# The first two gate/up blocks of a two-layer decoder as plain products in two token halves, and another order of the seven products of the 2x2 form

## The chip, the cores and the metric

The kernel runs on one core of one Trainium2 chip. The metric is the device time of one execution in microseconds (us), the median of three runs. The engines are named as the profile names them: PE does matmuls (PEld loads their weights), DVE, ACT and POOL do elementwise work, SP issues the DMAs from HBM. Matmuls write into PSUM banks; everything else lives in SBUF.

## The reference

Two layers over 512 tokens of width 1024. A layer is a token mixer, a LayerNorm over the residual sum, a SwiGLU feed-forward, a second LayerNorm, and a gated input embedding. All of it is fp32. The change touches the seam between the mixer's LayerNorm and the feed-forward's first product:

```python
x = layer_norm(DEEPNORM_ALPHA * x + h, ln_mix_g[i], ln_mix_b[i])          # h: the mixer's output, o @ w_o
x = layer_norm(DEEPNORM_ALPHA * x + swiglu_ffn(x, ffn_w_in[i], ffn_w_down[i]), ln_ffn_g[i], ln_ffn_b[i])
...
def swiglu_ffn(x, w_in, w_down):
    h = x @ w_in                       # (512 x 1024) @ (1024 x 5632)
    g, u = h[..., :D_FF], h[..., D_FF:]    # D_FF = 2816
    return (jax.nn.silu(g) * u) @ w_down
```

Layer 0 mixes by latent attention, layer 1 by a gated linear recurrence (HGRN2); both end with a product `o @ w_o` of 1024 x 1024.

## The kernel before, in words

**Precision.** Every fp32 operand is split into a high and a low part (`split`, lines 177 to 179: the high part by ACT, the low part by a subtraction on DVE, or on POOL where the caller says so), and a product is three matmuls (`mm3`, lines 190 to 195: high by high, high by low, low by high). So there are no single matmuls in what follows, only threes.

**The mixer's last product** (`out_proj`) runs over the four 128-token tiles t = 0 to 3, with tokens on the partitions. After the second 512 columns of a tile comes its LayerNorm: the sums (L318), mean (L324, L325), squared deviations on ACT (L326), the reciprocal root on POOL (`rstd`, L203: the power -0.5 of a 128x1 tile), and two passes over the tile in two halves each (L331, L335). Each half is then put on a list. `flush` takes the list: four PE transposes into one bank (L297), and the `sink` of `Winograd` makes the operands of the next product from that bank. `rows` calls `flush` after the matmuls of the next token tile, so tile t's transposes stand on PE behind tile t+1's matmuls. What is left on the list after the last tile (tile 2's and tile 3's halves) is flushed inside `gate_up`.

**gate/up** computes 22 blocks j of 128 gate and 128 up columns each, transposed (the 128 columns on the partitions, the 512 tokens along the row). Gate and up together, and the two token halves, make a 2x2 product of 2x2 quarters over the 1024 inner columns, and it is done with seven quarter products where eight would be plain. With A11, A12 (inner halves of tokens 0 to 255) and A21, A22 (of tokens 256 to 511), the sink makes S1 = A21 + A22, S2 = S1 - A11, S3 = A11 - A21 and S4 = A12 - S2; `prep(j)` (L380 to L401) loads the block's two 128x1024 weight units ra and rb and makes T1 (L389), half of T3 (L390), T2 (L391) and T4 (L392), each with its split. `product` is 12 matmuls of 128x256. A block is thus 84 matmuls.

The functions are recorded instruction by instruction; `prep(j)` is called ahead of block j, and a scheduler places the recorded work on the engines by its dependencies and by the tile pools. A tile of a pool must be free before its next owner may be written: raw weights have 3 buffers, whi and wlo 5 each, the middle-sized tiles `ma` and `mb` 5 each, PSUM has 3 banks `ps`, 2 `sc`, 2 `tp`, 1 `wg`. On an engine, instructions run in the order that the program gives.

**The seam.** Blocks 0 and 1 are written as generators that take turns: A11 and A12 of block 0, then `flush` (tile 2), the same of block 1 with `flush` (tile 3), A22 of both, and then the rest of both. A11 and A12 need tokens 0 to 255 alone, so they may run before tiles 2 and 3 are through their LayerNorm. From block 2 on the order is A11, S1, A12, S2, A22, S4, S3. Products into one bank accumulate: A11 with S2 and S3 into A; S1 with S4 into C. A copy of the bank (L416, ACT) is taken between them, and the sums with the copies (L424, L451, L454, L455 on DVE), the two silus on ACT (L425, L456) and the two products on POOL (L452, L457) make the block's 128 rows of h.

## Time and profile before

| what | us |
|---|---|
| median of three runs | 1347.09 |
| lowest and highest | 1346.31, 1347.42 |
| the profiled execution's own time | 1346.94 |
| its span, from the first to the last instruction | 1345.2 |
| PE busy in the span | 1286.0 (96%) |
| DVE, ACT, POOL busy | 905.9, 615.2, 328.3 |

The mean granted TensorE clock is 0.984 of full speed. Over the whole span PE is the engine that is nearly always busy, but an average hides stages; what the change touches are two short stretches, one per layer, where the mixer ends and gate/up begins: about 177 to 263 us and, 724.7 us later, 902 to 988 us. "Idle before" a row is the time for which its engine waited ahead of that instruction, and the arrow names what released it. Rows with a line of `mm3` (L193 to L195) say which product they belong to by the operand and the bank.

### The profile page before, as it was taken

To read this page: it belongs to the slowest core of one execution; us is meant where nothing else is said; L and a number is where in the kernel's file an instruction comes from. 1 tells how busy PE (TensorE), PEld (TensorE's weight loads), DVE (VectorE), ACT (ScalarE), POOL (GpSimd) and SP (SyncE) were. 2 spreads that over 40 slices of the span, in tenths; PEclk is the share of its full clock that TensorE was granted. 3 is DMA by queue.
4 is the path that set the end of the run, shared out by engine and by line. 5 is a ranking of instruction groups with operands and counts; after the bars stand their busy time and mean duration, and the time that the engine had idled before them with its cause. 6 is when DMAs were issued, how large, how long until landed. Compare 5 with 4: busy or idle time off the path is not lost.

```text
span 1345.2 us, 20010 instructions
## 1 busy us (share of the span) xinstructions
PE 1286.0 (96%) x7852; PEld 1144.8 (85%) x7852; DVE 905.9 (67%) x1396; ACT 615.2 (46%) x1080; POOL 328.3 (24%) x259
## 2 busy tenths in 40 slices
PE   8999978899999999999999999996899999999998
PEld 8787867899999888888888887886899999888887
DVE  7988398889884433753377776369789895633473
ACT  6666255555654333533334434235455554422352
POOL 0200034566552000100002220023566663100000
PEclk9999998999999999999999999997999999999999
DMA  6213102333332432331422220321333332433321
GB/s 220 79 48 126 47 32 95 110 111 95 110 110 71 142 101 95 97 119 64 126 62 64 63 63 29 129 72 39 126 95 98 122 96 64 157 96 105 97 91 51
DMA packets 36095, 125.00 MB, mean 93 GB/s; under 512 B 4384, under 2 KB 4640, under 8 KB 35744
## 3 DMA queue, kind: packets, MB, share of 16 engines
q1 hardware_dynamic: 36000, 123.71, 28.4%
q8 instruction: 62, 1.02, 0.3%
q14 instruction: 33, 0.27, 0.1%
HBM read 121.60 MB, written 2.10 MB: 92 GB/s over the span
## 4 chain that ended last, share of the span: by engine, by line
PE 82%; DVE 9%; issue 3%; POOL 3%; ACT 2%; DMA 1%; SPq 0%; DVEq 0%; POOLq 0%; ACTq 0%
PE ps L194 18%; PE ps L193 18%; PE ps L195 18%; PE sc L193 3%; PE sc L194 3%; PE sc L195 3%; PE wg L194 3%; PE wg L195 3%; PE wg L193 3%; PE tp L297 2%; DVE wlo L179 2%; PE sc L803 2%; PE tp L195 1%; PE tp L193 1%; PE tp L194 1%
## 5 line engine op out<-in xcount | busy, mean ns | idle before, releaser
L179 DVE TENSOR_TENSOR wlo<-raw,whi 128x1024 fp32r<-128x1024 f32 (+1 forms) x167 | 204.7, 1228 | 83.2 <-ACT whi L178 81.2
L193 PE MATMUL ps<-big,whi 128*128 128x256 f32 (+1 forms) x688 | 217.7, 316 | 20.8 <-ACT big L178 6.0
L178 ACT ACTIVATE whi<-raw 128x1024 fp32r<-128x1024 f32 (+1 forms) x171 | 177.1, 1038 | 111.2 <-PE ps L194 52.2
L195 PE MATMUL ps<-big,wlo 128*128 128x256 f32 (+1 forms) x688 | 216.5, 315 | 1.2 <-DVE wlo L179 1.2
L194 PE MATMUL ps<-big,whi 128*128 128x256 f32 (+1 forms) x688 | 215.1, 313 | 2.5 <-DVE big L179 2.5
L193 PE MATMUL ps<-whi,big 128*128 128x512 f32 (+2 forms) x440 | 171.0, 389 | 0.0
L195 PE MATMUL ps<-whi,big 128*128 128x512 f32 (+2 forms) x440 | 168.7, 383 | 0.0
L194 PE MATMUL ps<-wlo,big 128*128 128x512 f32 (+2 forms) x440 | 168.4, 383 | 0.0
L193 PEld LDWEIGHTS ps<-big,whi 128*128 128x128 f32 x688 | 133.8, 194 | 28.1 <-ACT big L178 6.6
L194 PEld LDWEIGHTS ps<-big,whi 128*128 128x128 f32 x688 | 133.7, 194 | 8.5 <-DVE big L179 3.1
L195 PEld LDWEIGHTS ps<-big,wlo 128*128 128x128 f32 x688 | 133.7, 194 | 6.8 <-DVE wlo L179 1.6
L203 POOL TENSOR_TENSOR rr<-rv,mhalf 128x1 f32<-128x1 f32 (+2 forms) x28 | 26.8, 958 | 424.7 <-DVE rv L201 424.7
L195 PEld LDWEIGHTS ps<-whi,big 128*128 128x128 f32 x440 | 83.1, 189 | 15.5
L179 DVE TENSOR_TENSOR ma<-big,ma 128x512 fp32r<-128x512 f32 x40 | 28.5, 717 | 100.4 <-ACT ma L178 100.4
L194 PEld LDWEIGHTS ps<-wlo,big 128*128 128x128 f32 x440 | 83.3, 189 | 14.4
L193 PEld LDWEIGHTS ps<-whi,big 128*128 128x128 f32 x440 | 83.2, 189 | 14.3
L390 POOL TENSOR_TENSOR ma<-raw,raw 128x512 f32<-128x512 f32 x44 | 87.8, 1994 | 0.0
L179 DVE TENSOR_TENSOR mb<-ma,mb 128x1024 fp32r<-128x1024 f32 x44 | 76.8, 1744 | 15.0 <-PE wg L194 15.0
L178 ACT ACTIVATE ma<-big 128x512 fp32r<-128x512 f32 x40 | 25.2, 630 | 122.6 <-PE wg L195 120.4
L389 POOL TENSOR_TENSOR ma<-raw 128x512 f32<-128x512 f32 x44 | 60.9, 1383 | 79.3 <-DVE wlo L179 63.4
L391 DVE TENSOR_TENSOR ma<-ma,raw 128x512 f32<-128x512 f32 x44 | 65.6, 1490 | 19.1 <-POOL ma L389 16.6
L457 POOL TENSOR_TENSOR big<-part,part 128x256 f32<-128x256 f32 x40 | 59.7, 1493 | 54.8 <-ACT part L456 54.8
(299 smaller groups left out, 3273.3 us busy)
## 6 DMA issues: line engine op xcount, KB each, us to landing
raw<-ffn_w_in SPq DMA_DIRECT2D x88, 512.0 KB, 3.6
raw<-ffn_w_down SPq DMA_DIRECT2D x44, 512.0 KB, 3.5
raw<-ple_w_gate SPq DMA_DIRECT2D x16, 512.0 KB, 3.5
raw<-hgrn_w_fq SPq DMA_DIRECT2D x16, 512.0 KB, 3.5
raw<-mla_w_o SPq DMA_DIRECT2D x8, 512.0 KB, 3.5
big<-ln SPq DMA_DIRECT2D x8, 512.0 KB, 4.8
raw<-hgrn_w_v SPq DMA_DIRECT2D x8, 512.0 KB, 4.7
raw<-hgrn_w_g SPq DMA_DIRECT2D x8, 512.0 KB, 3.5
```

What stands on the lines that cost most here:

```text
L178: self.nc.scalar.activation(hi, src, AF.Copy)
L179: (eng or self.nc.vector).tensor_tensor(out=lo, in0=src, in1=hi.bitcast(F32), op=ALU.subtract)
L193: mm(ps, a[0], b[0], start=start, stop=False, skip_group_check=more)
L194: mm(ps, a[0], b[1], start=False, stop=False, skip_group_check=more)
L195: mm(ps, a[1], b[0], start=False, stop=stop, skip_group_check=more)
L203: nc.gpsimd.tensor_tensor(out=r, in0=v, in1=self.mhalf[:, :n], op=ALU.pow)
L297: self.nc.tensor.transpose(out=ps[:, c * P:(c + 1) * P], in_=src[:, c * P:(c + 1) * P], identity=self.ident)
L389: nc.gpsimd.tensor_tensor(out=ta[:, up], in0=rb[:, up], in1=rb[:, lo], op=ALU.subtract)
L390: nc.gpsimd.tensor_tensor(out=ta[:, lo], in0=rb[:, lo], in1=ra[:, lo], op=ALU.subtract)
L391: v.tensor_tensor(out=tb[:, lo], in0=ta[:, up], in1=ra[:, lo], op=ALU.add)
L457: nc.gpsimd.tensor_tensor(out=h[:, N:], in0=u1, in1=g1, op=ALU.mult)
L803: nc.tensor.matmul(ps[:, c * P:(c + 1) * P], X[:, c * P:(c + 1) * P], pair_view(cs[0][:, :, 1, :], cs[1][:, :, 0, :]), start=True, stop=True)
```

## The change

`plain(h, w, half)` computes one token half of one block without the 2x2 form: gate and up, eight 128-wide inner pieces each, three matmuls of 128x256 for a piece, so 48 matmuls for a half and 96 for a block, where the 2x2 form has 84. Blocks 0 and 1 are computed so: tokens 0 to 255 of block 0, `flush`, the same of block 1, `flush`, then tokens 256 to 511 of both. Their weights come as four `unit`s whose low parts are made on POOL; `prep` is called for blocks 2 to 21 only. Since plain products of tokens 256 to 511 need A21, which the 2x2 form doesn't, the sink also splits A21 (one more ACT and one more DVE instruction of 128x512 for tiles 2 and 3 each). The sink's last subtraction, S4, goes from POOL to DVE. The LayerNorm parameters of the mixer stand in two `ma` tiles in place of a 14-slot pool's slot; the freed slot holds the A21 split. From block 2 on the order of products is A11, A12, S1, S2, A22, S4, S3.

Lines of the kernel after are 1 to 18 higher than before: L193 to L195 become L194 to L196, L203 becomes L204, L179 becomes L180, L331 and L335 become L334 and L338, L389 to L392 become L392 to L395, L451 becomes L453.

```diff
--- before.py
+++ after.py
@@ -106,14 +106,15 @@
         self.b = b
         two = lambda: [b.slot([P, 2, 4, 256], F32R) for _ in range(2)]
         self.a1, self.s13, self.s24 = two(), two(), two()
-        self.a22 = b.slot([P, 2, 4, 256], F32R)
+        self.a2 = [b.slot([P, 2, 4, 256], F32R) for _ in range(2)]
         self.raw = [b.mid([P, 4, 256]) for _ in range(2)]
         self.at = {}
 
     def __call__(self, name):
 
-        if name == "A22":
-            return self.a22[:, 0], self.a22[:, 1]
+        if name in ("A21", "A22"):
+            z = self.a2[name == "A22"]
+            return z[:, 0], z[:, 1]
         z, n = {"A11": (self.a1, 0), "A12": (self.a1, 1), "S1": (self.s13, 0), "S3": (self.s13, 1),
                 "S2": (self.s24, 0), "S4": (self.s24, 1)}[name]
         return z[0][:, n], z[1][:, n]
@@ -125,6 +126,7 @@
             b.split(self.a1[0][:, n, :, cs], self.a1[1][:, n, :, cs], ps)
             nc.scalar.activation(self.raw[n][:, :, cs], ps, AF.Copy)
             return
+        b.split(self.a2[n][:, 0, :, cs], self.a2[n][:, 1, :, cs], ps)
         if n == 0:
             a21 = b.small([P, 4, P], tag="t2", bufs=T2)
             nc.scalar.activation(a21, ps, AF.Copy)
@@ -136,8 +138,7 @@
         sy = b.mid([P, 2, 4, P], tag="mb")
         nc.vector.tensor_tensor(out=sx[:, 0], in0=ps, in1=a21, op=ALU.add)
         nc.vector.tensor_tensor(out=sy[:, 0], in0=ps, in1=sx[:, 1], op=ALU.subtract)
-        b.split(self.a22[:, 0, :, cs], self.a22[:, 1, :, cs], ps)
-        nc.gpsimd.tensor_tensor(out=sy[:, 1], in0=self.raw[1][:, :, cs], in1=sy[:, 0], op=ALU.subtract)
+        nc.vector.tensor_tensor(out=sy[:, 1], in0=self.raw[1][:, :, cs], in1=sy[:, 0], op=ALU.subtract)
         b.split(self.s13[0][:, :, :, cs], self.s13[1][:, :, :, cs], sx)
         b.split(self.s24[0][:, :, :, cs], self.s24[1][:, :, :, cs], sy)
 
@@ -306,11 +307,13 @@
         self.pend = []
 
 
-    def ln_params(self, idx):
-        gb = self.slot([P, 2, D])
+    def ln_params(self, idx, slot=False):
+        if slot:
+            z = self.slot([P, 2, D])
+        gb = (z[:, 0], z[:, 1]) if slot else (self.mid([P, D]), self.mid([P, D]))
         for n in range(2):
-            self.nc.sync.dma_start(gb[:, n], self.i["ln"][2 * idx + n])
-        return gb[:, 0], gb[:, 1]
+            self.nc.sync.dma_start(gb[n], self.i["ln"][2 * idx + n])
+        return gb
 
     def ln_half(self, x, t, n, ps, st):
 
@@ -405,13 +408,27 @@
                 self.mm3(ps[:, :N], [z[:, kc * P:(kc + 1) * P] for z in t], [z[:, kc] for z in s],
                          kc == 0 and not more, kc == 3, more)
 
-        def block(j):
-            w = prep(j)
+        def out(j):
             if j < 20 and j % 4 == 0:
                 hT.append(self.slot([P, 4, S]))
             elif j == 20:
                 hT.append(self.mid([P, 2, S]))
-            h = hT[j // 4][:, j % 4]
+            return hT[j // 4][:, j % 4]
+
+        def plain(h, w, half):
+
+            ps = [self.bank(), self.bank()]
+            for q in range(2):
+                for kc in range(KC):
+                    self.mm3(ps[q][:, :N], [z[:, kc * P:(kc + 1) * P] for z in w[q]],
+                             [z[:, kc % 4] for z in xT(f"A{half + 1}{kc // 4 + 1}")], kc == 0, kc == KC - 1)
+            g = self.small([P, N], tag="part", bufs=7)
+            nc.scalar.activation(g, ps[0][:, :N], AF.Silu)
+            v.tensor_tensor(out=h[:, half * N:(half + 1) * N], in0=ps[1][:, :N], in1=g, op=ALU.mult)
+
+        def block(j):
+            w = prep(j)
+            h = out(j)
             part = lambda: self.small([P, N], tag="part", bufs=7)
             copy = lambda dst, src: nc.scalar.activation(dst, src[:, :N], AF.Copy)
             A, B = self.bank(), self.bank("sc")
@@ -419,34 +436,19 @@
             product(A, xT("A11"), w["B11"])
             copy(g0, A)
 
-            def p2():
-                product(B, xT("A12"), w["B21"])
-                v.tensor_tensor(out=g0, in0=B[:, :N], in1=g0, op=ALU.add)
-                nc.scalar.activation(g0, g0, AF.Silu)
-
-            def p4():
-                d = self.bank("wg")
-                product(d, xT("A22"), w["T4"])
-                g1 = part()
-                copy(g1, d)
-                return g1
-
-            if j < 2:
-                p2()
-                self.flush()
-                yield
-                g1 = p4()
-                yield
+            product(B, xT("A12"), w["B21"])
+            v.tensor_tensor(out=g0, in0=B[:, :N], in1=g0, op=ALU.add)
+            nc.scalar.activation(g0, g0, AF.Silu)
             C = self.bank()
             u0, u1 = part(), part()
             product(C, xT("S1"), w["T1"])
             copy(u1, C)
-            if j >= 2:
-                p2()
             product(A, xT("S2"), w["T2"], True)
             copy(u0, A)
-            if j >= 2:
-                g1 = p4()
+            d = self.bank("wg")
+            product(d, xT("A22"), w["T4"])
+            g1 = part()
+            copy(g1, d)
             product(C, xT("S4"), w["B22"], True)
             v.tensor_tensor(out=u0, in0=C[:, :N], in1=u0, op=ALU.add)
             nc.gpsimd.tensor_tensor(out=h[:, :N], in0=u0, in1=g0, op=ALU.mult)
@@ -455,20 +457,21 @@
             v.tensor_tensor(out=u1, in0=A[:, :N], in1=u1, op=ALU.add)
             nc.scalar.activation(g1, g1, AF.Silu)
             nc.gpsimd.tensor_tensor(out=h[:, N:], in0=u1, in1=g1, op=ALU.mult)
-            yield
-
-        first = [block(0), block(1)]
-        for _ in range(3):
-            for b in first:
-                next(b)
+
+
+        hs = [out(j) for j in range(2)]
+        ws = [[self.unit(win[j, q], True) for q in range(2)] for j in range(2)]
+        for half in range(2):
+            for j in range(2):
+                plain(hs[j], ws[j], half)
+                self.flush()
         for j in range(2, NF):
-            for _ in block(j):
-                pass
+            block(j)
         return hT
 
     def ffn(self, l, x, xT, ln):
         hT = self.gate_up(l, xT)
-        gb = self.ln_params(ln)
+        gb = self.ln_params(ln, True)
         yT = Pair(self)
         acc = [(self.bank(f), self.bank(g)) for f, g in (("tp", "tp"), ("sc", "sc"), ("ps", "ps"), ("ps", "wg"))]
         NL = 3
```

Two places show how the instructions stand. The first is POOL at the seam of layer 0. rr is the reciprocal root of a LayerNorm (in these rows the four tiles of the mixer's, in order), wlo a weight unit's low part, ma<-raw the two subtractions of `prep`, mb<-ma the sink's S4. Before:

```order
L203 TENSOR_TENSOR rr_1944<-rv_1942,mhalf 128x1
L203 TENSOR_TENSOR rr_1998<-rv_1996,mhalf 128x1
L389 TENSOR_TENSOR ma_2128<-raw_2121 128x512
L390 TENSOR_TENSOR ma_2128<-raw_2121,raw_2120 128x512
L389 TENSOR_TENSOR ma_2208<-raw_2201 128x512
L390 TENSOR_TENSOR ma_2208<-raw_2201,raw_2200 128x512
L203 TENSOR_TENSOR rr_2052<-rv_2050,mhalf 128x1
L140 TENSOR_TENSOR mb_2097<-ma_1752,mb_2097 128x512
L203 TENSOR_TENSOR rr_2114<-rv_2112,mhalf 128x1
L140 TENSOR_TENSOR mb_2190<-ma_1752,mb_2190 128x512
```

and now:

```order
L180 TENSOR_TENSOR wlo_2128<-raw_2125,whi_2127 128x1024
L204 TENSOR_TENSOR rr_1946<-rv_1944,mhalf 128x1
L204 TENSOR_TENSOR rr_2000<-rv_1998,mhalf 128x1
L204 TENSOR_TENSOR rr_2054<-rv_2052,mhalf 128x1
L180 TENSOR_TENSOR wlo_2134<-raw_2131,whi_2133 128x1024
L180 TENSOR_TENSOR wlo_2140<-raw_2137,whi_2139 128x1024
L180 TENSOR_TENSOR wlo_2146<-raw_2143,whi_2145 128x1024
L392 TENSOR_TENSOR ma_2395<-raw_2388 128x512
L393 TENSOR_TENSOR ma_2395<-raw_2388,raw_2387 128x512
L204 TENSOR_TENSOR rr_2118<-rv_2116,mhalf 128x1
```

The first row's low part is plain block 0's. Three more of them now stand behind tile 2's reciprocal root (rr_2054); then come block 2's two subtractions (L392, L393), and tile 3's reciprocal root (rr_2118) stands behind these. Before, tile 3's (rr_2114) had only S4 of tile 2 ahead of it. raw_2388 is the second weight unit of block 2; its buffer is the one that plain block 1's first unit (raw_2137, read by wlo_2140) leaves.

The second place is DVE in the same stretch, from tile 2's LayerNorm to tile 3's. big_1741 holds tiles 2 and 3 of the residual, tp are transposed tiles, ps_2004 and now ps_2006 tile 2's last product, ps_2060 tile 3's. Before:

```order
L391 TENSOR_TENSOR ma_2129<-ma_2128,raw_2120 128x512
L179 TENSOR_TENSOR ma_2134<-raw_2121,ma_2134 128x512
L318 SCALAR_TENSOR_TENSOR big_1741,lnst_1758<-big_1741,ps_2004 128x512
L392 TENSOR_TENSOR ma_2129<-ma_2129,raw_2120 128x512
L179 TENSOR_TENSOR big_1745<-tp_2029,big_1744 128x4x128
L179 TENSOR_TENSOR big_1745<-tp_2037,big_1744 128x4x128
L324 TENSOR_TENSOR lnst_1758<-lnst_1758 128x1
L325 TENSOR_SCALAR lnst_1758<-lnst_1758 128x1
L179 TENSOR_TENSOR wlo_2138<-ma_2128,whi_2137 128x1024
L201 TENSOR_SCALAR rv_2050<-lnst_1758 128x1
L331 SCALAR_TENSOR_TENSOR big_1741<-big_1741,lnst_1758,big_1753 128x512 x2
L335 SCALAR_TENSOR_TENSOR big_1741<-big_1741,rr_2052,big_1753 128x512 x2
```

and now:

```order
L321 SCALAR_TENSOR_TENSOR big_1741,lnst_1760<-big_1741,ps_2006 128x512
L327 TENSOR_TENSOR lnst_1760<-lnst_1760 128x1
L328 TENSOR_SCALAR lnst_1760<-lnst_1760 128x1
L180 TENSOR_TENSOR big_1745<-tp_2031,big_1744 128x4x128
L180 TENSOR_TENSOR big_1745<-tp_2039,big_1744 128x4x128
L202 TENSOR_SCALAR rv_2052<-lnst_1760 128x1
L334 SCALAR_TENSOR_TENSOR big_1741<-big_1741,lnst_1760,ma_1754 128x512 x2
L338 SCALAR_TENSOR_TENSOR big_1741<-big_1741,rr_2054,ma_1755 128x512 x2
L321 SCALAR_TENSOR_TENSOR big_1741,lnst_1761<-big_1741,ps_2060 128x512
L327 TENSOR_TENSOR lnst_1761<-lnst_1761 128x1
L328 TENSOR_SCALAR lnst_1761<-lnst_1761 128x1
L180 TENSOR_TENSOR big_1750<-tp_2085,big_1750 128x4x128
```

Before, block 0's weight work (L391, ma_2134, L392, wlo_2138) stood among tile 2's steps; now its sums, mean and passes follow each other with only tile 1's two splits between them, and its own splits (tp_2085) come after tile 3's mean. Further on the same engine, the second half of tile 3's second pass and block 2's preparation now stand thus:

```order
L338 SCALAR_TENSOR_TENSOR big_1741<-big_1741,rr_2118,ma_1755 128x512
L427 TENSOR_TENSOR big_2124<-ps_2150,part_2199 128x256
L180 TENSOR_TENSOR big_1750<-tp_2202,big_1750 128x4x128
L180 TENSOR_TENSOR wlo_2392<-raw_2387,whi_2391 128x1024
L134 TENSOR_TENSOR mb_2211<-ma_1752,tp_2202 128x512
L180 TENSOR_TENSOR big_1751<-tp_2213,big_1751 128x4x128
L139 TENSOR_TENSOR mb_2211<-tp_2213,t_420_2209 128x512
L140 TENSOR_TENSOR mb_2220<-tp_2213,mb_2211 128x512
L427 TENSOR_TENSOR big_2124<-ps_2229,part_2278 128x256
L141 TENSOR_TENSOR mb_2220<-ma_1753,mb_2220 128x512
L180 TENSOR_TENSOR big_1747<-mb_2211,big_1746 128x8x128
L394 TENSOR_TENSOR ma_2396<-ma_2395,raw_2387 128x512
```

The row that waits for tile 3's reciprocal root (rr_2118) has plain block 0's product with silu (L427), block 2's first low part (wlo_2392) and the whole sink of tile 3 (tp_2202, tp_2213) behind it, and only then comes block 2's T2 (L394).

On PE, tile 2's transposes now stand directly behind tile 3's 24 matmuls; then come plain block 0's 48 matmuls, 14 of plain block 1's in layer 0 (24 in layer 1), tile 3's first four transposes, the rest of that half with the other four among it, and the 96 matmuls of the second halves. Before, 11 matmuls of block 0 stood ahead of tile 2's transposes, and tile 3's stood behind A11 and A12 of blocks 0 and 1.

## The prediction

> **What bounds the kernel now.** I read the page's shares first: PE is busy for 96% of the span, so only what shortens PE's work or its waits can help. Then the busy time by stretches, from block 0's first matmul to block 4's last, and from there to block 20's, for each layer.
>
> ```profile
> 183.80:262.80 79.00, 61.26 (x437) 58.95 (x436) 68.56 (x81) 41.55 (x68) 36.96 (x26) 0.87 0.24 81
> 262.80:423.00 160.20, 160.20 (x1337) 160.20 (x1336) 128.98 (x150) 87.55 (x153) 86.97 (x59) 1.00 0.30 93
> 908.50:987.30 78.80, 61.27 (x438) 59.01 (x438) 68.19 (x81) 40.32 (x67) 37.05 (x26) 0.87 0.25 82
> 987.30:1148.00 160.70, 160.70 (x1342) 160.70 (x1341) 129.34 (x150) 87.56 (x153) 87.00 (x60) 1.00 0.30 93
> ```
>
> The columns are length, then busy time and count for PE, PEld, DVE, ACT and POOL, then the granted clock. In the steady stretch PE never rests: 160.20/1337 = 0.120 us for a matmul of 256 columns, 10.1 us for a block of 84. The first five blocks are 420 matmuls, 50.3 us at that pace, and 16 transposes (0.13 us each, four in 0.63 with the tail, next fence) make 2.1. They take 79.0 us, so **26.6 us are lost** in layer 0 and 78.80 - 52.4 = 26.4 in layer 1. The clock, 0.87, is part of it. Who is waited for, over the whole span and at the seam:
>
> ```profile
> PE tp L297 <- DVE big L335: 15.8, 6, 4.2
> PE ps L193 <- ACT part L416: 7.4, 4, 2.6
> PE ps L193 <- ACT big L178: 6.0, 2, 3.3
> PE ps L193 <- DVE part L451: 5.6, 4, 1.9
> PE ps L194 <- DVE big L179: 2.5, 2, 1.3
> ...
> 177.85 0.63 PE L297 MATMUL tp<-ident,big 128*128 128x128 f32 x4 [0.95 <-DVE big L335]
> 188.61 0.92 PE L297 MATMUL tp<-ident,big 128*128 128x128 f32 x4 [3.35 <-DVE big L335]
> 200.07 1.94 PE L297 MATMUL tp<-ident,big 128*128 128x128 f32 x8 [4.16 <-DVE big L335]
> 204.67 0.58 PE L193 MATMUL ps<-big,whi 128*128 128x256 f32 x1 [2.65 <-ACT big L178]
> 206.99 0.58 PE L194 MATMUL ps<-big,whi 128*128 128x256 f32 x1 [1.25 <-DVE big L179]
> 226.98 0.39 PE L193 MATMUL ps<-big,whi 128*128 128x256 f32 x1 [1.47 <-DVE part L451]
> 236.84 0.58 PE L193 MATMUL ps<-big,whi 128*128 128x256 f32 x1 [2.64 <-ACT part L416]
> 254.10 0.38 PE L193 MATMUL ps<-big,whi 128*128 128x256 f32 x1 [1.94 <-DVE part L451]
> ```
>
> The first three wait for a LayerNorm pass (L335) before tiles 1, 2 and 3 can be transposed, the next two for the sink's splits, the last three, blocks later, for a bank to be read. The seven that lie inside the stretch add to 17.5 us. The rest of the 26.6 is clock:
>
> ```profile
> 185.40:188.80 3.40, 0.19 (x2) 0.22 (x3) 2.96 (x4) 2.01 (x2) 2.16 (x2) 1.00 0.00 0
> 188.80:192.20 3.40, 3.40 (x18) 3.40 (x17) 3.40 (x7) 1.82 (x3) 0.00 (x0) 0.50 0.00 0
> 233.20:236.60 3.40, 1.00 (x9) 0.80 (x7) 3.40 (x5) 2.50 (x4) 0.75 (x1) 1.00 0.03 7
> 236.60:240.00 3.40, 3.15 (x15) 3.16 (x15) 2.04 (x3) 1.36 (x4) 0.84 (x1) 0.50 0.82 301
> ```
>
> After a stretch in which PE sat idle for 2.4 of 3.4 us the next 3.4 us were granted half the clock: 1.7 us more per such stall. [...]
>
> **Out_proj's end and tile 2.** What makes L335 late now is company, not work:
>
> ```profile
> 164.72 0.69 DVE L318 SCALAR_TENSOR_TENSOR big<-big,ps 128x512 f32<-128x512 f32 x1 [1.33 <-PE ps L195]
> 168.53 1.41 DVE L335 SCALAR_TENSOR_TENSOR big<-big,rr,big 128x512 f32<-128x512 f32 x2
> 174.24 3.46 DVE L335 SCALAR_TENSOR_TENSOR big<-big,rr,big 128x512 f32<-128x512 f32 x2
> 182.33 1.23 DVE L179 TENSOR_TENSOR wlo<-ma,whi 128x1024 fp32r<-128x1024 f32 x1 [0.76 <-ACT whi L178]
> 174.06 1.42 POOL L389 TENSOR_TENSOR ma<-raw 128x512 f32<-128x512 f32 x1
> 175.44 1.72 POOL L390 TENSOR_TENSOR ma<-raw,raw 128x512 f32<-128x512 f32 x1
> 196.89 1.00 POOL L203 TENSOR_TENSOR rr<-rv,mhalf 128x1 f32<-128x1 f32 x1 [2.96 <-DVE rv L201]
> ```
>
> Tile 0's LayerNorm runs undisturbed: 5.2 us from L318 at 164.72 to 169.94. Tile 1's second pass takes 3.46 instead of 1.41 while POOL's L389 and L390 run beside it. In the change prep of block 0 is gone from there: the 0.95 us at 177.85 go, and out_proj ends at 183.80 - 0.95, about 182.8. Tile 2's matmuls ended at 177.85 - 0.95 = 176.9, its LayerNorm is through 5.2 later, at 182.1, and DVE's row for it has no weight split inside. Its transposes stand at 182.8: **no wait** (3.35 now, and the half clock after it).
>
> **Tile 3.** Plain block 0's first half, 48 matmuls, follows: 1.0 for eight transposes and 5.7 for the matmuls, to 189.6, then 14 of block 1 in layer 0 (24 in layer 1): tile 3's transposes are wanted at 191.3 (192.5). They won't be ready. Tile 3's last matmul ends at 182.8, and alone its LayerNorm would be done at 188; but its reciprocal root stands on POOL behind three low parts and behind L392 and L393 of block 2, and these behind a load. POOL made such parts in out_proj:
>
> ```profile
> 157.70 2.40 POOL L179 TENSOR_TENSOR wlo<-raw,whi 128x1024 fp32r<-128x1024 f32 x1 [33.61 <-ACT whi L178]
> 208.54 1.28 POOL L389 TENSOR_TENSOR ma<-raw 128x512 f32<-128x512 f32 x1 [2.69 <-DMA raw<-ffn_w_in]
> 232.66 1.29 POOL L390 TENSOR_TENSOR ma<-raw,raw 128x512 f32<-128x512 f32 x1
> 260.86 2.27 POOL L390 TENSOR_TENSOR ma<-raw,raw 128x512 f32<-128x512 f32 x1
> raw<-ffn_w_in SPq DMA_DIRECT2D x88, 512.0 KB, 3.6
> 161.07 1.06 ACT L178 ACTIVATE whi<-raw 128x1024 fp32r<-128x1024 f32 x1 [2.08 <-DMA raw<-ffn_w_in]
> ```
>
> From tile 2's reciprocal root, at about 181 (tile 2's L318 at 177 and some 3.7 as in tile 0): 2.40 for plain block 0's second unit, 2.40 for block 1's first, which frees the buffer that block 2's second weight unit is loaded into: 185.8, with ACT's high part (1.06 us) and the sum's slack about 186.5. The load lands 3.6 later, 190.1, the third low part is done before. L392 and L393 take 1.3 to 2.3 each; 3.9 for both puts them at 194.2, the root (1.00) at 195.2, the second pass (1.41) at 196.6. So PE waits **5.3 us in layer 0 and 4.1 in layer 1**, and either is long enough for a half-clock stretch: 1.7 more each. Bounds: with both POOL steps at their lowest (2.6) and the load straight after the part, 194.5; with the two at 2.3 and DVE delaying the parts, 199. That is 3.2 to 7.7 in layer 0.
>
> **The second halves and blocks 2 to 4.** After the transposes 34 matmuls are left of block 1's half, then come 96 with operands that are then there (A21's two extra splits a tile, of 128x512 each, so about half of a unit's 1.06 and 1.23, lie behind tile 3's transposes while 34 matmuls, 4.1 us, run): no wait counted, up to 2.65 + 1.25 if not. These 96 matmuls are the cover for prep. What ends waits later is in DVE's queue:
>
> ```profile
> 213.98 0.68 DVE L391 TENSOR_TENSOR ma<-ma,raw 128x512 f32<-128x512 f32 x1
> 223.50 1.77 DVE L391 TENSOR_TENSOR ma<-ma,raw 128x512 f32<-128x512 f32 x1 [1.89 <-POOL ma L389]
> 232.73 1.76 DVE L391 TENSOR_TENSOR ma<-ma,raw 128x512 f32<-128x512 f32 x1 [1.19 <-POOL ma L389]
> 240.49 1.21 DVE L391 TENSOR_TENSOR ma<-ma,raw 128x512 f32<-128x512 f32 x1 [1.85 <-POOL ma L389]
> 251.97 1.73 DVE L391 TENSOR_TENSOR ma<-ma,raw 128x512 f32<-128x512 f32 x1 [1.19 <-POOL ma L389]
> ```
>
> These are T2's starts for blocks 2 to 6, 9.5 us apart on average, a train hardly faster than PE's 10.1. In the change T2 of block 2 stands behind tile 3's sink, which needs the transposes of 196.6 and twelve matmuls: with the half clock some 4 us to the second bank, then 0.68 twice, a subtraction, two splits of 1.2, or up to twice that where POOL works beside them: about 206, **8 us earlier than 213.98**. At such steps (some shorter, as from 232.73 to 240.49) the next ones start near 216, 224, 232 and 240. PE is at the second halves' end at 196.6 + 1.0 + 4.1 + 1.7 + 11.5 = 214.9, so block 2 finds all of its operands. But a block's L453 has the T2 of a later block ahead of it (block 2's stands behind block 4's, block 3's behind block 6's), and the next block's first matmul needs the bank that L453 reads: the same wait as at 226.98 and 254.10. Replaying this I get waits of 1.25, 2.9 and 1.2 us up to block 4, **5.35 us**; nothing if the train is 3 us quicker, about 11 if it is 3 us slower.
>
> **The sum, layer 0.** 182.8 + 444 matmuls (24 more) x 0.120 = 53.2, + 2.1 transposes + 5.3 + 1.7 + 5.35 = 250.4, against 262.8: 12.4 saved. The 2.9 us of extra matmuls are in it. Layer 1: the wait is 1.2 shorter, 13.3 saved against 987.3 - 724.7 = 262.6. Together 25.7. **From block 2 on** the new order leaves the copy of A the same two products (2.9 us) before S2 as before; A12's bank is used sooner and C has one product more until S4. ACT is busy 87.55 of 160.20 and DVE 128.98, so I take nothing for it; a stall of 0.3 us in each of the 40 blocks would be 12. **S4 on DVE** costs 0.7 to 1.4 us twice a layer there, before T2 (in the 206), and spares POOL 1.3 twice. **LayerNorm parameters in two `ma` tiles** of five: the loads come well ahead of tile 0 and I take nothing; a late one would cost up to a load's landing, 3.6 us by the weights' row.
>
> So 1346.94 - 25.7 = 1321.2 for an execution like the profiled one, which lies 0.15 us from the median of three: **1321 us**.
>
> **The rivals.**
>
> *Quicker POOL and load.* If block 2's load lands by 187 and the parts run shorter beside a quiet DVE, tile 3's root is 3 to 4 us earlier, the wait falls to about 1.5, no stretch at half clock follows, and T2's train starts 3 us sooner. Against it: the row at 157.70 has 2.40, and DVE will have work beside these parts too. 2 x (3.8 + 1.7) = 11 less: 1310. With no stall left the bound is 1346.94 - 53 + 5.8 - 1.9 = 1298.
>
> *The train catches up as slowly as now.* If T2 of block 2 starts only 3 us earlier, near 211, because DVE's splits take twice their time beside POOL's work, as the pass at 174.24 did, the later waits take back most: block 4 ends 3 to 4 us earlier than now in each layer, 1339.
>
> *All of it is given back.* With T2 at 214 again and 2.9 us more matmuls hidden under waits: 1347, no difference.
>
> *Slower: the new order stalls each block.* A12 right behind A11 puts L440's sum and the silu ahead of the copies of C and A in ACT's queue. If S2 then waits for A's copy, the price is paid 40 times and not twice: the row of L416 (7.4 us in four waits, 1.85 each) shows that PE does wait there when ACT is late. Above 25.7/40 = 0.64 us a block nothing of the gain is left; at 0.8 it is 1353. Against it: the steady stretch has no PE idle time now and ACT is busy for 55% of it.
>
> **How the numbers follow.** The forecast (1314 to 1331) 0.60; quicker POOL (1298 to 1314) 0.14; slow train (1331 to 1344) 0.17; no difference 0.03; slower 0.06. The range 1306 to 1336 takes half of the second case and half of the third, and leaves out about 0.2. A change of under 0.2% (2.7 us) is about what a measurement of this kernel can't tell from none: faster 0.91, same 0.03, slower 0.06.
>
> **What would show it.** Tile 2's transposes without a wait at about 183; tile 3's with 3 to 8 us, released by L338, with POOL's L392 and L393 directly ahead of the root and the landing of ffn_w_in ahead of these; a granted clock of 0.50 just behind; T2 of block 2 at about 206; first matmuls of blocks 3 to 5 waiting for L453; block 4's end near 250 and, in layer 1, 974; the steady stretch at 0.120 a matmul. Wrong would be: idle time on PE between products from block 5 on, a wait for the A21 splits, or T2 of block 2 not before 211.

## The result

The changed kernel takes 1327.06 us (median of four runs, 1324.79 to 1328.05) against 1347.26 (1346.31 to 1348.4) for the kernel before beside it: a ratio of 0.9847, 95% interval 0.983 to 0.9864. That is 20 us less, where 25.7 were forecast (1321, range 1306 to 1336). The profiled execution has a span of 1325.4 us, 19.8 less than the 1345.2 of before.

The busy time by stretches, for layer 0 and layer 1: from the end of the mixer's product to block 4's last matmul, and from there on to block 20's. The columns are length, then busy time and count of PE, PEld, DVE, ACT and POOL, the granted clock, DMA share and GB/s.

```profile
182.80:250.10 67.30, 57.35 (x457) 56.39 (x458) 59.45 (x70) 35.36 (x55) 30.47 (x20) 0.97 0.32 103
250.10:411.30 161.20, 161.20 (x1346) 161.20 (x1345) 123.18 (x150) 87.40 (x153) 83.64 (x60) 1.00 0.30 92
896.20:964.80 68.60, 59.22 (x457) 58.59 (x458) 59.51 (x72) 34.15 (x54) 30.28 (x20) 0.93 0.30 100
964.80:1126.00 161.20, 161.20 (x1346) 161.20 (x1345) 120.95 (x149) 87.44 (x153) 78.38 (x59) 1.00 0.30 92
```

The steady stretch is as it was: 161.20/1346 = 0.120 us a matmul, with PE never idle. The seams are shorter, in spite of 24 more matmuls each. Block 4 of layer 0 ends at 250.1 instead of 262.8, **12.7 us** earlier. The seam of layer 1 begins 11.3 us earlier than before (896.2 against 182.8 + 724.7 = 907.5) and its block 4 ends at 964.7 instead of 987.3, so it saves another 22.6 - 11.3 = **11.3 us**. That would be 24.0. But 12.7 had shrunk to 11.3 between the two seams, and 22.6 shrinks to 19.8 by the end: **1.4 and 2.8 us are lost again**, nearly all of it in a place that the prediction passed over, block 21: from its first matmul to the first of the next stage it took 14.1 us in layer 0 and 13.8 in layer 1 before, and takes 15.3 and 16.5 now. The waits of PE over the whole span:

```profile
PE ps L194 <- ACT part L433: 9.3, 5, 3.8
PE tp L298 <- DVE big L338: 9.0, 4, 3.5
PE ps L196 <- DVE wlo L180: 5.0, 2, 2.5
PE ps L194 <- ACT whi L179: 1.4, 2, 0.7
PE ps L194 <- DVE part L453: 1.1, 1, 1.1
```

and by time (layer 0's seam, layer 1's, and block 21 of layer 1; block 21 of layer 0 has the same two waits, 0.72 and 2.49 us, at 415.11 and 418.10):

```profile
183.79 0.63 PE L298 MATMUL tp<-ident,big 128*128 128x128 f32 x4 [1.03 <-DVE big L338]
195.35 0.63 PE L298 MATMUL tp<-ident,big 128*128 128x128 f32 x4 [3.51 <-DVE big L338]
218.39 0.38 PE L194 MATMUL ps<-big,mb 128*128 128x256 f32 x1 [0.54 <-ACT part L433]
224.97 0.38 PE L194 MATMUL ps<-big,whi 128*128 128x256 f32 x1 [2.01 <-ACT part L433]
235.79 0.38 PE L194 MATMUL ps<-big,ma 128*128 128x256 f32 x1 [1.94 <-ACT part L433]
244.21 0.39 PE L194 MATMUL ps<-big,mb 128*128 128x256 f32 x1 [0.97 <-ACT part L433]
897.15 0.63 PE L298 MATMUL tp<-ident,big 128*128 128x128 f32 x4 [1.03 <-DVE big L338]
909.88 0.80 PE L298 MATMUL tp<-ident,big 128*128 128x128 f32 x4 [3.48 <-DVE big L338]
940.95 0.39 PE L194 MATMUL ps<-big,whi 128*128 128x256 f32 x1 [1.11 <-DVE part L453]
949.51 0.58 PE L194 MATMUL ps<-big,ma 128*128 128x256 f32 x1 [3.85 <-ACT part L433]
1129.81 0.38 PE L194 MATMUL ps<-big,whi 128*128 128x256 f32 x1 [0.72 <-ACT whi L179]
1132.80 0.58 PE L196 MATMUL ps<-big,wlo 128*128 128x256 f32 x1 [2.49 <-DVE wlo L180]
```

Three groups are seen: the LayerNorm of tiles 2 and 3 (L338), the banks of blocks 2 to 4 (L433, L453), and block 21's T1, whose high part comes 0.72 and whose low part 2.49 us late.

### The profile page after: what moved, and what is told of

It is laid out like the page before. It is cut to its first block, busy times and chain, and to the rows that moved or that the text cites. A ratio compares the mean times of both kernels' runs of the same rounds, so it can differ in the third digit from the quotient of the medians.

```text
span 1325.4 us, 20024 instructions
## 1 busy us (share of the span) xinstructions
PE 1282.8 (97%) x7900; PEld 1144.1 (86%) x7900; DVE 869.8 (66%) x1372; ACT 605.5 (46%) x1060; POOL 306.5 (23%) x247
## 4 chain that ended last, share of the span: by engine, by line
PE 81%; DVE 9%; issue 4%; POOL 2%; ACT 2%; DMA 1%; SPq 0%; DVEq 0%; POOLq 0%; ACTq 0%
PE ps L194 18%; PE ps L196 18%; PE ps L195 18%; PE sc L194 3%; PE sc L195 3%; PE sc L196 3%; PE wg L195 2%; PE wg L194 2%; PE wg L196 2%; PE tp L298 2%; PE sc L806 2%; PE tp L194 2%; PE tp L195 2%; PE tp L196 2%; DVE wlo L180 1%
## 5 line engine op out<-in xcount | busy, mean ns | idle before, releaser
L180 DVE TENSOR_TENSOR wlo<-raw,whi 128x1024 fp32r<-128x1024 f32 (+1 forms) x163 | 201.4, 1238 | 82.0 <-ACT whi L179 79.6
L194 PE MATMUL ps<-big,whi 128*128 128x256 f32 (+1 forms) x768 | 239.7, 312 | 4.6 <-ACT part L433 2.0
L196 PE MATMUL ps<-big,wlo 128*128 128x256 f32 (+1 forms) x768 | 239.1, 311 | 5.0 <-DVE wlo L180 5.0
L195 PE MATMUL ps<-big,whi 128*128 128x256 f32 (+1 forms) x768 | 237.8, 310 | 0.0
L179 ACT ACTIVATE whi<-raw 128x1024 fp32r<-128x1024 f32 (+1 forms) x175 | 181.0, 1039 | 111.8 <-PE ps L195 53.5
L194 PE MATMUL ps<-whi,big 128*128 128x512 f32 (+2 forms) x440 | 170.7, 388 | 0.3 <-DVE ma L601 0.3
L196 PE MATMUL ps<-whi,big 128*128 128x512 f32 (+2 forms) x440 | 168.3, 383 | 0.0
L195 PE MATMUL ps<-wlo,big 128*128 128x512 f32 (+2 forms) x440 | 168.0, 382 | 0.0
L196 PEld LDWEIGHTS ps<-big,wlo 128*128 128x128 f32 x768 | 149.1, 194 | 10.6 <-DVE wlo L180 5.4
L194 PEld LDWEIGHTS ps<-big,whi 128*128 128x128 f32 x768 | 149.1, 194 | 10.2 <-ACT part L433 2.2
L195 PEld LDWEIGHTS ps<-big,whi 128*128 128x128 f32 x768 | 149.2, 194 | 5.4
L204 POOL TENSOR_TENSOR rr<-rv,mhalf 128x1 f32<-128x1 f32 (+2 forms) x28 | 27.8, 994 | 419.6 <-DVE rv L202 419.6
L196 PEld LDWEIGHTS ps<-whi,big 128*128 128x128 f32 x440 | 82.8, 188 | 15.5
L194 PEld LDWEIGHTS ps<-whi,big 128*128 128x128 f32 x440 | 82.9, 188 | 14.7 <-ACT whi L179 0.5
L195 PEld LDWEIGHTS ps<-wlo,big 128*128 128x128 f32 x440 | 83.0, 189 | 14.5
L180 DVE TENSOR_TENSOR mb<-ma,mb 128x1024 fp32r<-128x1024 f32 x40 | 65.2, 1630 | 44.7 <-PE wg L195 44.7
L180 DVE TENSOR_TENSOR ma<-big,ma 128x512 fp32r<-128x512 f32 x40 | 28.5, 717 | 100.4 <-ACT ma L179 100.4
L179 ACT ACTIVATE ma<-big 128x512 fp32r<-128x512 f32 x40 | 25.2, 630 | 122.5 <-PE wg L196 120.4
L392 POOL TENSOR_TENSOR ma<-raw 128x512 f32<-128x512 f32 x40 | 54.4, 1361 | 99.1 <-DMA raw<-ffn_w_in 80.6
L393 POOL TENSOR_TENSOR ma<-raw,raw 128x512 f32<-128x512 f32 x40 | 69.0, 1725 | 0.0
L180 POOL TENSOR_TENSOR wlo<-raw,whi 128x1024 fp32r<-128x1024 f32 x12 | 29.6, 2476 | 152.3 <-ACT whi L179 152.3
L196 PE MATMUL ps<-whi,ma 128*128 128x512 f32 x164 | 64.2, 392 | 0.0
```

The lines of the kernel that those rows point to most:

```text
L179: self.nc.scalar.activation(hi, src, AF.Copy)
L180: (eng or self.nc.vector).tensor_tensor(out=lo, in0=src, in1=hi.bitcast(F32), op=ALU.subtract)
L194: mm(ps, a[0], b[0], start=start, stop=False, skip_group_check=more)
L195: mm(ps, a[0], b[1], start=False, stop=False, skip_group_check=more)
L196: mm(ps, a[1], b[0], start=False, stop=stop, skip_group_check=more)
L204: nc.gpsimd.tensor_tensor(out=r, in0=v, in1=self.mhalf[:, :n], op=ALU.pow)
```

## The experiments

Each was timed beside the kernel before, and the ratio is to that.

### The order of the products, undone and alone

The plain first blocks kept, the order of before from block 2 on:

```diff
             product(A, xT("A11"), w["B11"])
             copy(g0, A)
-            product(B, xT("A12"), w["B21"])
-            ...
             product(C, xT("S1"), w["T1"])
             copy(u1, C)
+            product(B, xT("A12"), w["B21"])
+            ...
             product(A, xT("S2"), w["T2"], True)
```

> The change with one part undone: from block 2 on the products stand in the order of before (A11, S1, A12, S2, A22, S4, S3); the plain first blocks stay. Theory (the gain is the plain blocks', the order moves little): within 3 us of the change, 1324 to 1330 us. Rival (the new order costs the 4.2 us that the change lost at block 21 of the two layers): 1322 to 1324. Rival (the new order is a good part of the gain): 1332 or more.

Measured: 1328.93 us, ratio 0.9864 (0.9849 to 0.9879), not to be told from the change, as the theory had it. The first rival is right about the place and wrong about the time: block 21 takes 13.8 us in both layers here, 1.5 and 2.7 less than in the change, but in its profile block 21 of layer 0 also begins 5.5 us later. Of these 1.6 arose ahead of the seam, the rest between the seam and block 20, where PE waits 1.93 us for L453 in block 5, a wait that the change doesn't have. (In layer 1 that stretch is 0.8 us shorter.) And the other half alone, the new order in the kernel before:

```diff
-            product(C, xT("S1"), w["T1"])     # j >= 2: ahead of A12
-            copy(u1, C)
             product(B, xT("A12"), w["B21"])
             ...
+            product(C, xT("S1"), w["T1"])
+            copy(u1, C)
```

> The kernel before with one part of the change alone: from block 2 on the products stand as A11, A12, S1, S2, A22, S4, S3; blocks 0 and 1 in the 2x2 form as before. Theory (order moves little): 1344 to 1350 us. Rival (the order is a good part of the gain): 1341 or less. Rival (the new order costs at block 21): 1349 to 1352.

Measured: 1348.29 us, ratio 1.0006 (0.9997 to 1.0015): no difference that the time shows. In its profile block 21 takes 15.3 us in both layers, 1.2 and 1.5 more than before, and the seams are 0.5 and 0.7 shorter. So the order moves time from one place to another and brings nothing in sum. The gain belongs to the rest of the change, of which the plain blocks are the bulk; its smaller parts (S4 on DVE, LayerNorm's parameters in `ma` tiles) were not undone one by one.

### Who holds the copies

The trace names ACT's copies (L433) as what blocks 2 to 5 wait for. Here DVE makes them in blocks 2, 3 and 4:

```diff
-            copy = lambda dst, src: nc.scalar.activation(dst, src[:, :N], AF.Copy)
+            copy = lambda dst, src: v.tensor_copy(dst, src[:, :N]) if j in (2, 3, 4) else nc.scalar.activation(dst, src[:, :N], AF.Copy)
```

> The change, but the copies of the accumulating banks in blocks 2, 3 and 4 are made by DVE instead of ACT. Theory (the waits of blocks 2 to 5, 6.1 us in layer 0 and 4.0 with a half-clock stretch in layer 1, come from the copies standing in ACT's queue behind splits of later blocks): these waits fall to under 3 us a layer, 1317 to 1322 us. Rival (the copies only show that block 2's and 3's operands are late, the wait moves to the operands or the sums L453): 1325 to 1329 us.

Measured: 1329.22 us, ratio 0.9865 (0.9848 to 0.9881). The theory fell: the rival's time. PE still waits for these copies, now of DVE, 4.9 us in layer 0 and 6.2 in layer 1. The change's own rows around the longest such wait, 949.51, say why. First DVE, then ACT:

```profile
942.88 1.21 DVE L394 TENSOR_TENSOR ma<-ma,raw 128x512 f32<-128x512 f32 x1 [1.32 <-POOL ma L392]
944.01 2.31 DVE L180 TENSOR_TENSOR wlo<-raw,whi 128x1024 fp32r<-128x1024 f32 x1
947.38 0.41 DVE L440 TENSOR_TENSOR part<-sc,part 128x256 f32<-128x256 f32 x1
947.82 0.42 ACT L441 ACTIVATE part<-part 128x256 f32<-128x256 f32 x1 [1.49 <-DVE part L440]
949.09 0.64 ACT L433 ACTIVATE part<-ps 128x256 f32<-128x256 f32 x2
```

Block 3's sum with the first copy (L440) stands in DVE's queue behind the preparation of a later block, which itself waits for POOL; ACT's silu (L441) waits for that sum, and the copies stand behind the silu. On DVE the copies stand behind the same preparation. The name in the wait is the last link; the cause is the train of preparations, whose place in the queue is ahead of work that PE needs.

### Tile 3's reciprocal root freed of block 2

Block 2's two subtractions, which stand ahead of tile 3's reciprocal root on POOL, are made by DVE:

```diff
+            e = v if j == 2 else nc.gpsimd
-            nc.gpsimd.tensor_tensor(out=ta[:, up], in0=rb[:, up], in1=rb[:, lo], op=ALU.subtract)
-            nc.gpsimd.tensor_tensor(out=ta[:, lo], in0=rb[:, lo], in1=ra[:, lo], op=ALU.subtract)
+            e.tensor_tensor(out=ta[:, up], in0=rb[:, up], in1=rb[:, lo], op=ALU.subtract)
+            e.tensor_tensor(out=ta[:, lo], in0=rb[:, lo], in1=ra[:, lo], op=ALU.subtract)
```

> The change, but block 2's two subtractions L392 and L393 are made by DVE instead of POOL, so tile 3's reciprocal root has only the three low parts ahead of it on POOL. Theory (the root stands behind these two and their load): the wait for tile 3's second pass, 3.7 us in each layer, falls to under 1 us and the half-clock stretch of about 1.6 us behind it goes, but the train of blocks 2 to 4 gets no earlier and takes back half: 1320 to 1324 us. Rival (the low parts alone hold the root as long, or DVE is the late one): 1326 to 1330 us.

Measured: 1323.77 us, ratio 0.9828 (0.9813 to 0.9842), 3.3 us less than the change, though the two intervals still overlap. Tile 3's wait, measured from the start of one PE instruction to that of the next less the usual distance, falls from 3.7 to 1.5 us in layer 0 and from 3.6 to 1.4 in layer 1, and no half-clock stretch follows (the granted clock is 1.00 in the 10 us behind it in both layers). So the two subtractions did hold tile 3. What is left of the wait doesn't come from the root's standing behind the low parts. Tile 3's root in this run:

```profile
189.20 0.99 POOL L204 TENSOR_TENSOR rr<-rv,mhalf 128x1 f32<-128x1 f32 x1 [1.12 <-DVE rv L202]
```

POOL has sat idle for 1.12 us when it starts, and what it waits for is DVE, which has rows of tile 2's sink ahead of L202 and of both passes. By which way the subtractions held tile 3 is looked at with the prediction below. And as expected the later waits take back a part: those up to block 4 in layer 0 grow from 6.1 to 7.7 us by the same measure, with a half-clock stretch that wasn't there (0.50 over 244.00 to 247.40).

### What paces the train: a fourth raw buffer

```diff
-        raw = self.wp.tile([P, 1024], F32, tag="raw", bufs=3, name=self.nm("raw"))
+        raw = self.wp.tile([P, 1024], F32, tag="raw", bufs=4, name=self.nm("raw"))
-T2 = 4
+T2 = 2
```

> The change with four raw weight buffers instead of three; for room, the buffers of a small scratch tile (t2) go from four to two. Theory (the train of block preparations after the seam is paced by its loads, which wait for a raw buffer that the block before leaves late): block 3's and 4's loads start earlier, the waits of blocks 2 to 5 (6.1 and 5.3 us) fall to under 3 in each layer, 5 to 8 us faster than the control with two t2 buffers, so 1319 to 1323 if that control is at 1327. Rival (DVE's and ACT's queues pace the train): within 2 us of the control.

> Control for the run with four raw buffers: the change with two t2 buffers instead of four and nothing else. Every theory expects the change's time or somewhat more, 1326 to 1335 us.

Measured: 1323.91 us with four raw buffers (ratio 0.9824, 0.9809 to 0.9839), 1334.83 with two t2 buffers alone (0.9909, 0.9893 to 0.9926). (The fourth buffer is given at the two other places that share this pool as well.) So t2's room costs 8 us elsewhere, 7 of them ahead of the first seam, and the fourth raw buffer is worth 10.9; in the profiles the way from the start of the seam to the end of block 4 is 4.7 us shorter in layer 0 and 5.4 in layer 1. The starts of T2 for blocks 2 and 3 in layer 0, first the control, then with four buffers (both begin the seam some 7 us later than the change):

```profile
211.65 0.69 DVE L394 TENSOR_TENSOR ma<-ma,raw 128x512 f32<-128x512 f32 x1
220.26 1.77 DVE L394 TENSOR_TENSOR ma<-ma,raw 128x512 f32<-128x512 f32 x1 [1.19 <-POOL ma L392]
```

```profile
204.66 0.69 DVE L394 TENSOR_TENSOR ma<-ma,raw 128x512 f32<-128x512 f32 x1
218.53 0.68 DVE L394 TENSOR_TENSOR ma<-ma,raw 128x512 f32<-128x512 f32 x1
```

Blocks 4 to 6 follow at 228.75, 236.61 and 246.17 in the control and at 226.28, 232.90 and 240.90 with four. With three buffers DVE waits for POOL at each block from block 3 on, and POOL for a load: in the change, which has three as well, L392 of blocks 3 to 7 in layer 0 starts 3.6 to 4.0 us after its unit's load is issued (the median to landing is 3.6). With four, DVE's waits are gone up to block 5 and the train is 1.7 to 7 us ahead. PE's waits in blocks 2 to 4 fall from 4.8 and 5.3 us in the control's two layers to 1.4 and 1.7. So the loads' buffers hold the train back. They do it in two ways, which this run doesn't part: from block 3 to block 6 a step takes 7.5 us on average in place of 8.6, and block 2's T2 comes 7 us earlier, since in DVE's queue it now stands ahead of tile 3's sink and no longer behind it.

### More cover: a third plain block

```diff
+        h, w = out(2), [self.unit(win[2, q], True) for q in range(2)]
+        for half in range(2):
+            plain(h, w, half)
-        for j in range(2, NF):
+        for j in range(3, NF):
             block(j)
```

> The change with block 2 as a plain block too (both token halves after those of blocks 0 and 1), 12 matmuls or 1.4 us more a layer. Theory (what is lost behind tile 3's transposes is that PE catches up with the train, and 96 matmuls more give the train 11.5 us): the waits of blocks 2 to 5 (6.1 in layer 0, 5.3 and a half-clock stretch in layer 1) fall to about 2 a layer, 1318 to 1323 us. Rival (the train starts as much later as the cover is longer, so the waits stay): 1328 to 1332 us.

Measured: 1319.91 us, ratio 0.9789 (0.9775 to 0.9804), 7 us less than the change for 2.9 us of matmuls more. The later waits fall from 6.1 and 5.3 to 1.6 and 0.3 us. Tile 3's stay: 10.0 us for L338 over the span, where the change has 9.0.

### The low parts on DVE

```diff
-        ws = [[self.unit(win[j, q], True) for q in range(2)] for j in range(2)]
+        ws = [[self.unit(win[j, q]) for q in range(2)] for j in range(2)]
```

> The change with the low parts of the four plain weight units made by DVE instead of POOL. Theory (tile 2's second pass takes 3.5 us instead of 1.4 because POOL makes low parts beside it, and the three parts hold block 2's load): tile 2's wait of 1.2 us goes, tile 3's falls to about 2, but DVE has some 5 us more before tile 3's sink: 1323 to 1327 us. Rival (DVE is the bottleneck of the seam): 1329 to 1335 us.

Measured: 1324.09 us, ratio 0.9824 (0.981 to 0.9839). The interval overlaps the change's. Tile 2's wait is gone and tile 3's is 2.2 us. Here too tile 3's root finds POOL idle, for 3.49 us, and waits for DVE's L202. The later waits, up to block 5, are 5.5 and 6.3 us, with a half-clock stretch in either layer (0.50 over 233.80 to 237.20 and 946.20 to 949.60).

### Block 21

The old order in block 21 alone, the rest as in the change:

```diff
+            if j < NF - 1:
+                p2()
             C = self.bank()
             u0, u1 = part(), part()
             product(C, xT("S1"), w["T1"])
             copy(u1, C)
+            if j == NF - 1:
+                p2()
```

(`p2` is A12 with its sum and silu.)

> The change, with the product order of before (A11, S1, A12, S2, ...) in block 21 alone. Theory (in the new order the two waits of block 21, 0.9 and 2.7 us, stand 0.2 us apart and bring half a clock of 1.7 to 3.4 us behind them; in the old order they stand 1.5 us apart around A12's matmuls and mostly don't): the same 3.5 us of waits in each layer, but the granted clock of the 13 us from there at 1.00, and 3 to 5 us less: 1322 to 1325 us. Rival (the half clock there is chance, a matter of where the wait falls): 0.74 to 0.87 again, 1325 to 1328 us.

Measured: 1325.15 us, ratio 0.9838 (0.9823 to 0.9853). The interval overlaps the change's, and the time lies on the border between theory and rival, so it doesn't decide. The profile does for the place: 13 us from block 21's T1 on, in layers 0 and 1 of the change, then in layer 1 of this kernel with its two waits.

```profile
413.11:426.11 13.00, 9.79 (x67) 9.38 (x66) 11.04 (x15) 8.31 (x15) 1.91 (x3) 0.87 0.65 239
1127.81:1140.81 13.00, 9.79 (x57) 9.38 (x56) 10.57 (x13) 7.60 (x13) 1.78 (x2) 0.74 0.66 238
```

```profile
1129.73 0.39 PE L194 MATMUL ps<-big,whi 128*128 128x256 f32 x1 [1.99 <-ACT whi L179]
1132.74 0.38 PE L196 MATMUL ps<-big,wlo 128*128 128x256 f32 x1 [1.20 <-DVE wlo L180]
1126.46:1139.46 13.00, 9.81 (x80) 9.41 (x79) 11.49 (x15) 8.39 (x15) 3.40 (x4) 1.00 0.61 216
```

The waits are as long together (0.72 + 2.49 and 1.99 + 1.20), and PE is busy as long, but 80 matmuls fit where 57 did. In the old order A12's matmuls stand between the two waits; in the new one A12 is already done and they come 0.2 us apart. Over the kernels of this study the new order shows 0.74 or 0.87 there in 16 of 16 places (two layers each of eight profiles), and block 21 takes 15.1 to 16.5 us; the old order shows 1.00 in 6 of 10, and the block takes 13.8 to 14.1 us in nine of them and 16.0 in one. In the kernel before, it is 1.00 in layer 1 and 0.87 in layer 0. So in these kernels the half clock there came with the order, mostly; the old order didn't exclude it. The longest single wait differs too, 2.49 against 1.99 us, and no run tells whether that or the distance between the two counts.

Block 21 gives back 1.5 and 2.7 us in this run's profile, but the span is only 2.8 us shorter than the change's. A part goes again at the seam of layer 0, where a wait of 1.95 us at 236.48 was followed by half the clock (0.51 over 238.00 to 241.40), and one of 1.94 at 235.79 in the change by full speed (1.00 over 237.78 to 241.19).

### Together

Three plain blocks and block 21 in the old order, and then the low parts of all three on DVE as well, which leaves nothing but LayerNorm's own roots ahead of tile 3's on POOL:

```diff
-        ws = [[self.unit(win[j, q], True) for q in range(2)] for j in range(2)]
+        ws = [[self.unit(win[j, q]) for q in range(2)] for j in range(2)]
-        h, w = out(2), [self.unit(win[2, q], True) for q in range(2)]
+        h, w = out(2), [self.unit(win[2, q]) for q in range(2)]
```

> Three plain blocks, and block 21 in the old order. Theory: the two gains add, 1319.9 less 3 to 5: 1315 to 1317 us. Rival (the half clock at block 21 is chance): 1318 to 1321 us.

> Three plain blocks with all their low parts made by DVE, and block 21 in the old order. Tile 3's reciprocal root then stands behind nothing but tile 2's on POOL, and block 3's load comes late enough not to matter. Theory (with the train hidden by a third plain block, the remaining waits at the seam, 1.2 for tile 2 and 3.7 and a half-clock stretch for tile 3, are POOL's): they fall to under 2 in each layer, 4 to 8 us faster than three plain blocks with POOL's low parts, 1308 to 1313 us. Rival (DVE's 7 us more a layer delay tile 3's pass and the train as much): 1315 to 1320 us.

Measured: 1317.92 us (ratio 0.9781, 0.9766 to 0.9795) and **1311.23 us (0.9737, 0.9721 to 0.9753)**. The first is 2 us below three plain blocks, less than the 3 to 5 expected, since block 21's stretch was granted 0.87 and 0.74 again in its profile. The second beats both kernels: 35 us below the kernel before, and its interval lies wholly below the change's. PE's waits in it:

```profile
PE ps L194 <- ACT part L433: 4.0, 2, 3.3
PE ps L194 <- ACT whi L179: 4.0, 2, 2.0
PE tp L298 <- DVE big L338: 1.7, 2, 1.0
```

L338 is down to 1.7 us, from 10.0 with three plain blocks and POOL's low parts. The low parts that DVE now makes cost less than that: in blocks 3 to 5 one copy (L433) is 3.3 us late, in layer 1.

## Why the prediction was right, and where it wasn't

**Out_proj's end and tile 2: partly wrong.** Tile 2's transposes were to come without a wait. There is one of 1.03 us in each layer. The cause is the one named for the kernel before, in a new place. First DVE, then POOL:

```profile
180.09 3.55 DVE L338 SCALAR_TENSOR_TENSOR big<-big,rr,ma 128x512 f32<-128x512 f32 x2
184.28 1.62 DVE L327 TENSOR_TENSOR lnst<-lnst 128x1 f32<-128x1 f32 x1
180.67 7.59 POOL L180 TENSOR_TENSOR wlo<-raw,whi 128x1024 fp32r<-128x1024 f32 x3 [0.75 <-ACT whi L179]
```

POOL begins the three low parts 0.75 us after tile 2's root is out, while DVE is in the pass that needs the root. The first half of the pass takes 0.75 us, the second 2.89: it ends 0.55 us after the first low part. The prediction used 1.41 us for that pass, from a row without company, and had put POOL's parts at the same time. With the low parts on DVE the wait is gone.

**Tile 3: right about who holds it, wrong about the way, too large in size.** POOL's rows came as forecast, L392 and L393 behind the load and the root behind them:

```profile
189.44 1.69 POOL L392 TENSOR_TENSOR ma<-raw 128x512 f32<-128x512 f32 x1 [1.17 <-DMA raw<-ffn_w_in]
191.09 1.71 POOL L393 TENSOR_TENSOR ma<-raw,raw 128x512 f32<-128x512 f32 x1
192.76 1.53 POOL L204 TENSOR_TENSOR rr<-rv,mhalf 128x1 f32<-128x1 f32 x1
```

The three were put at 190.1 to 195.2 and came at 189.4 to 194.3. But the root isn't the last thing that the second pass (L338) waits for. DVE at the same time:

```profile
189.88 1.79 DVE L141 TENSOR_TENSOR mb<-ma,mb 128x512 f32<-128x512 f32 x1
191.59 2.29 DVE L180 TENSOR_TENSOR big<-mb,big 128x1024 fp32r<-128x1024 f32 x1
193.81 0.74 DVE L334 SCALAR_TENSOR_TENSOR big<-big,lnst,ma 128x512 f32<-128x512 f32 x1
194.47 0.74 DVE L338 SCALAR_TENSOR_TENSOR big<-big,rr,ma 128x512 f32<-128x512 f32 x1
```

DVE is never idle here. The second half of the first pass (L334) stands behind two rows of tile 2's sink and ends at 194.54, after the root (194.29). In layer 1 it is plainer:

```profile
906.14 1.54 POOL L204 TENSOR_TENSOR rr<-rv,mhalf 128x1 f32<-128x1 f32 x1
908.99 1.41 DVE L338 SCALAR_TENSOR_TENSOR big<-big,rr,ma 128x512 f32<-128x512 f32 x2
```

The root is out at 907.68 and the pass begins at 908.99, behind one more split of tile 2. The two sink rows in the fence take 1.79 and 2.29 us beside L392 and L393; where DVE makes the two subtractions later on, they take 0.68 and 1.22. That is 2.2 us less, the very amount by which tile 3's wait falls in that run. So L392 and L393 reach the pass by two ways, through the root, which they hold, and through DVE's queue, which they slow, and the second ended last in both layers. The run that moves them ends both at once and can't part them; the rows can. The prediction's chain had the root and then 1.41 us for the pass, and nothing for the sink rows that stand among the halves of tile 3's two passes. (Its sum is also 0.2 off: 190.1 and 3.9 make 194.0.)

PE waits 3.5 us in both layers, where 5.3 and 4.1 were forecast. The transposes needed only the first half of the pass, at 195.2 in layer 0; the prediction counted both. The granted clock, ahead of the transposes and behind them:

```profile
193.41:196.82 3.41, 1.47 (x13) 1.50 (x14) 3.41 (x5) 0.60 (x1) 0.88 (x1) 1.00 0.00 0
196.82:200.23 3.41, 3.41 (x18) 3.41 (x18) 2.91 (x6) 1.47 (x3) 0.00 (x0) 0.50 0.02 5
```

One stretch of 3.41 us at 0.50: the 1.7 us of the forecast.

**The later waits: right in size, right about the train, one link off.** T2's starts were put near 206, 216, 224, 232 and 240:

```profile
204.12 0.69 DVE L394 TENSOR_TENSOR ma<-ma,raw 128x512 f32<-128x512 f32 x1
...
239.24 1.77 DVE L394 TENSOR_TENSOR ma<-ma,raw 128x512 f32<-128x512 f32 x1 [2.30 <-POOL ma L392]
```

with 213.33, 221.82 and 229.69 between. The waits add to 5.5 us in layer 0 (5.35 forecast) and 5.0 in layer 1, there with a half-clock stretch at the one of 3.85 (0.50 over 947.75 to 954.58) that layer 0 doesn't have. The prediction held the sum L453 to be what is late; it is mostly the copies, behind the silu, behind L440. Both stand behind the same preparations in DVE's queue. That the waits belong to the train is shown from two sides: more cover (a third plain block) and a quicker train (a fourth raw buffer) each take most of them away, and a shorter wait ahead of them makes them longer.

**The sum.** Layer 0: 12.4 forecast, 12.7 measured. That these agree is in part luck, since the 1.0 us of tile 2 that were put at nothing are made up for by the 1.8 that were counted too much for tile 3. Layer 1: 13.3 forecast, 11.3 measured, for tile 2's 1.0 and the half-clock stretch. Among its signs the prediction gives 974 for block 4's end in layer 1; that leaves out what layer 0 saves. With the 12.4 of its own sum it would be 961.6, and it came at 964.7.

**The step that failed: nothing taken for the new order "from block 2 on".** In the steady stretch that holds: 0.120 us a matmul, and no wait. But block 21 is not like the others. Its T1 is late in every kernel here, and the order decides what lies between the two waits. It is there that 1.2 and 2.7 us of the forecast gain went, 3.9 of the 5.9 that are missing between the spans (25.7 forecast, 19.8 found); the other 2.0 are layer 1's seam. The prediction had that place neither as a term nor as a rival. The slower rival had the right suspect (the order) and the wrong place (each block). It doesn't follow that the old order would have been faster: undone everywhere, the new order's price at block 21 came back, and about as much was lost elsewhere.

Why T1 of block 21 is late at all was not tried. The trace shows the last link: its first subtraction on POOL (L392 at 411.41) stands behind block 20's product L454 (410.71), though its weights were asked for at 383.4.

**The extra matmuls** cost their 0.120 us each, and no run shows a further price: 24 in a layer, and 12 more with the third plain block, which still gained.

## What to carry to other kernels

When a start-up is late because operands come through a chain of small steps, plain work that needs only early operands is cheap cover: here 24 matmuls a layer, with the moves that went with them, bought about 12 us at each seam, and 12 more a layer another 7 us over both, their own cost taken off. But cover only moves PE along a train that has its own pace; ask what paces the train (here the raw buffers) before shortening any single wait, because a wait that is cut early comes back later in part. A small instruction's place in one queue is not the only way in which work on another engine can hold it: look at how long the rows ahead of it take in company (here 1.79 and 2.29 us where 0.68 and 1.22 were enough without). And where two waits are unavoidable, see what stands between them: two short idle times next to each other were dearer here (0.72 and 2.49 us, a granted clock of 0.74 over the 13 us from there) than two that add to the same 3.2 us but stood 1.5 us apart (1.99 and 1.20 us, 1.00).
